# First modulation pair in single chunks, norm squares summed on TensorE, first products chunk by chunk

## The chip, the core and the metric

The kernel runs on one NeuronCore of a Trainium2 chip. The metric is the device time of one execution in microseconds (us). The engines are TensorE (PE; its weight loads are shown apart as PEld), VectorE (DVE), ScalarE (ACT), GpSimd (POOL) and SyncE (SP), which issues most of the DMA transfers.

## What is computed

Two transformer-like blocks over 512 tokens of width 1024: the first with retention, a Fourier mix and a gated feed-forward layer, the second with a gated MLP, windowed attention and 16 experts. Everything that the change touches lies in the first steps of the first block:

```python
mod = silu(c) @ w_mod + b_mod                    # 6 x 1024 columns
sh1, sc1, ... = split(mod, 6)
h  = rms_norm(x, norm1_w) * (1 + sc1) + sh1      # 512 x 1024
hc = the same for ctx (256 x 1024), with c_ctx
...
gate_f = sigmoid(h @ w_branch_gate[:, 1024:] + b)    # the first product with h
k_ctx, v_ctx = hc @ w_in[:, K and V columns]
```

## The kernel before

Activations are held transposed: 128 partitions of the model width by 512 tokens, in 8 chunks `k` of the width. Every fp32 operand of a large product is split into a high part in the matmul format and the remainder, and a product is three matmuls of 128x128 by 128x512 (`mm3`, L222 to L224: weight-high by x-high, weight-high by x-low, weight-low by x-high). The order of instructions on each engine is the order in which the code is written; nothing is rescheduled.

The first stage brings in `xin` (8 chunks in 4 DMAs), then the first four weight blocks of the gate (`wraw`, items 0 to 3, split into high and low by ScalarE and VectorE: `cH`/`cL`, `wh`/`wl`) and the modulation weights. These come in pairs: `pair_load(kp)` issues four DMAs of 512 KB, which hold shift and scale of the chunks `2kp` and `2kp+1`; `pair_mm(kp)` multiplies them on TensorE by silu(c) and silu(c_ctx) (L450) and copies the result to SBUF on ScalarE (L454); `pair_fin(kp)` sums and transposes it with eight passes on TensorE (L461) and makes `mod1` and `A1` = (1 + scale) * norm weight on VectorE (L465, L467).

The norm of x squares the chunks on ScalarE (L360, L364), adds them up on VectorE (L367), sums over partitions on TensorE (`col_sums`, L336, a product with a column of ones), takes the reciprocal root on small tiles and broadcasts it with L348 into PSUM (`pB`). `norm_pre(k)` multiplies a chunk by `pB` on VectorE (L523); `start_norm(k)` then applies scale and shift on ScalarE (L528), takes the high part in a second ScalarE pass (L530) and the remainder on VectorE (L531).

`part(c, kp)` runs the products of weight block `c` with the two chunks of pair `kp`. `warm(n)` issues n throw-away matmuls (L478, two passes each) whose only effect is that TensorE is busy; the counts come from the table `WARM0`. After the last norm, the code splits two more weight blocks and sums the squares of the context (`c1[0]`, `c1[1]`: L360, L364, L367), and behind the last products of this stage TensorE makes the context's column sums (`c1[2]`, L336). From there TensorE goes straight on to the next four blocks of the gate.

## Time and profile before

| | us |
|---|---|
| median of 3 runs (lowest to highest) | 2325.15 (2323.64 to 2325.17) |
| the profiled execution | 2323.48 |
| its span in the trace | 2321.7 |
| TensorE busy in the span | 2223.4 (96%) |
| start of the first product with h | 22.90 |
| start of the context's column sums | 57.96 |

The profiled execution is 1.78 us longer than its span and 1.67 us shorter than the median of the runs. Times in the rows below count from the start of the span. Matmul durations overlap, so the pace of a run of matmuls is read from their starts or from the chain.

### The profile page before, as it was taken

The numbers are of one execution on the slowest core, as the hardware profiler recorded it, in microseconds if no ns is written. First come the engines' busy times: TensorE is split into PE (matmuls) and PEld (weight loads), VectorE is DVE, ScalarE is ACT, GpSimd is POOL, SyncE is SP. The second block draws the span as 40 slices with busy tenths as digits, with TensorE's granted clock in tenths as the row PEclk, the third lists the DMA queues.
The fourth block names the chain that finished last, engine by engine and source line by source line (L and its number), as shares of the span: only waits on it lengthen the run. The fifth ranks groups of instructions, "written<-read, shape, count | busy, mean of one in ns | idle before, by whom it ended". The sixth has DMA issues, their size and how long they took to land.

```text
span 2321.7 us, 27993 instructions
## 1 busy us (share of the span) xinstructions
PE 2223.4 (96%) x11118; PEld 1460.6 (63%) x11118; DVE 1061.7 (46%) x2064; ACT 658.6 (28%) x1034; POOL 164.8 (7%) x304
## 2 busy tenths in 40 slices
PE   8999999999999999999999999999999989888987
PEld 6788888878888888888976785434333323332333
DVE  4645675679787865524667552111211111111112
ACT  5532234344243545332466431000000000000002
POOL 0202010101112100002211000000000000000000
PEclk9999999999999999999999999999999999999999
DMA  8647254734456544235510498999999999999998
GB/s 321 229 162 211 87 155 157 260 118 152 156 192 207 165 144 127 82 114 162 153 42 19 142 362 351 417 421 432 431 430 431 432 432 431 430 432 431 431 428 348
DMA packets 95970, 616.79 MB, mean 266 GB/s; under 512 B 12832, under 2 KB 17568, under 8 KB 75680
## 3 DMA queue, kind: packets, MB, share of 16 engines
q1 hardware_dynamic: 77136, 558.63, 60.9%
q0 software_dynamic: 18704, 56.38, 8.2%
q8 instruction: 88, 1.44, 0.3%
q14 instruction: 42, 0.34, 0.0%
HBM read 590.05 MB, written 14.94 MB: 261 GB/s over the span
## 4 chain that ended last, share of the span: by engine, by line
PE 79%; DMA 17%; DVE 2%; ACT 2%; issue 1%; POOLq 0%; SPq 0%; DVEq 0%; ACTq 0%
DMA xr<-in_w_exp_dram 16%; PE mm L224 13%; PE mm L222 13%; PE mm L223 13%; PE pgu L1817 12%; PE py L1884 6%; PE ps L1700 3%; PE b L255 2%; PE b L254 2%; PE b L253 2%; PE sm L1361 1%; PE mm L1349 1%; PE b L222 1%; PE b L223 1%; PE b L224 1%; PE ps L1731 1%
## 5 line engine op out<-in xcount | busy, mean ns | idle before, releaser
L1817 PE MATMUL pgu<-xr,xt 128*64 128x512 f32 x2032 | 463.0, 599 | 33.1 <-DMA xr<-in_w_exp_dram 32.5
L222 PE MATMUL mm<-aH,wh 128*128 128x512 f32 (+1 forms) x1104 | 420.1, 381 | 2.3 <-ACT aH L380 2.3
L223 PE MATMUL mm<-aL,wh 128*128 128x512 f32 (+1 forms) x1104 | 417.3, 378 | 0.0
L224 PE MATMUL mm<-aH,wl 128*128 128x512 f32 (+1 forms) x1104 | 417.2, 378 | 0.1
L131 DVE TENSOR_TENSOR wl<-wraw,wh 128x1024 fp32r<-128x1024 f32 (+1 forms) x212 | 256.2, 1212 | 184.6 <-ACT wh L122 184.2
L1817 PEld LDWEIGHTS pgu<-xr,xt 128*64 128x64 f32 x2032 | 143.5, 137 | 298.2 <-issue 266.8
L122 ACT ACTIVATE wh<-wraw 128x1024 fp32r<-128x1024 f32 (+1 forms) x212 | 220.1, 1044 | 262.7 <-PE mm L223 182.3
L1884 PE MATMUL py<-xr,hTe 128*64 128x512 f32 x944 | 218.2, 608 | 21.7 <-DMA xr<-in_w_exp_dram 21.7
L222 PEld LDWEIGHTS mm<-aH,wh 128*128 128x128 f32 x1104 | 208.3, 189 | 41.0 <-ACT aH L380 2.6
L224 PEld LDWEIGHTS mm<-aH,wl 128*128 128x128 f32 x1104 | 208.3, 189 | 39.3 <-DVE wl L131 0.5
L223 PEld LDWEIGHTS mm<-aL,wh 128*128 128x128 f32 x1104 | 208.4, 189 | 37.9 <-DVE aL L383 0.4
L1884 PEld LDWEIGHTS py<-xr,hTe 128*64 128x64 f32 x944 | 67.6, 139 | 139.9 <-issue 124.4
L1855 DVE TENSOR_TENSOR eg<-pgu,eg 128x512 f32<-128x512 f32 x32 | 22.1, 692 | 208.0 <-PE pgu L1817 194.7
L1807 ACT ACTIVATE hTe<-pT 128x512 f32<-128x512 f32 x32 | 19.1, 598 | 334.4 <-PE pT L1806 334.4
L1735 DVE TENSOR_TENSOR aH<-ps,aH 128x512 f32<-128x512 f32 x56 | 38.7, 692 | 121.8 <-PE ps L1732 121.8
L1705 DVE TENSOR_SCALAR xt<-ps,B,mod 128x128 f32<-128x128 f32 x32 | 11.6, 405 | 162.7 <-PE ps L1700 162.7
L108 ACT ACTIVATE yh<-y 128x512 fp32r<-128x512 f32 x15 | 9.4, 629 | 225.2 <-DVE y L1899 211.2
L1899 DVE SCALAR_TENSOR_TENSOR y<-py,sw,g2B 128x512 f32<-128x512 f32 x15 | 11.3, 750 | 135.3 <-PE py L1884 135.3
L1700 PEld LDWEIGHTS ps<-sel,xtok 128*128 128x128 f32 x496 | 57.8, 192 | 24.3 <-issue 24.3
L282 POOL DMA_DIRECT2D mraw<-in_w_adaT_dram x96 | 51.6, 537 | 302.7 <-DVE mod L297 300.7
L222 PE MATMUL mm<-gH,wh 128*128 128x512 f32 x176 | 68.5, 389 | 0.0
L223 PE MATMUL mm<-gL,wh 128*128 128x512 f32 x176 | 68.5, 389 | 0.0
(494 smaller groups left out, 3117.3 us busy)
## 6 DMA issues: line engine op xcount, KB each, us to landing
xr<-in_w_exp_dram SPq DMA_DIRECT2D x66, 4096.0 KB, 29.9
xr<-in_w_exp_dram SPq DMA_DIRECT2D x30, 2048.0 KB, 13.9
xr<-in_w_exp_dram SPq DMA_DIRECT2D x55, 1024.0 KB, 9.7
mraw<-in_w_adaT_dram POOLq DMA_DIRECT2D x96, 256.0 KB, 2.9
wraw<-in_w_up_dram SPq DMA_DIRECT2D x44, 512.0 KB, 4.0
wraw<-in_w_kv_tok_dram SPq DMA_DIRECT2D x20, 512.0 KB, 4.2
wraw<-in_w_bg_dram SPq DMA_DIRECT2D x16, 512.0 KB, 3.7
mraw<-in_w_modT_dram POOLq DMA_DIRECT2D x32, 256.0 KB, 4.8
```

The costliest lines, as they stand in the source:

```text
L122: nc.scalar.activation(h[:, :sz], r[:, :sz], AF.Copy)
L131: nc.vector.tensor_tensor(*lows.pop(0), OP.subtract)
L222: nc.tensor.matmul(ps, wh, xh, start=first, stop=False)
L223: nc.tensor.matmul(ps, wh, xl, start=False, stop=False)
L224: nc.tensor.matmul(ps, wl, xh, start=False, stop=last)
L253: nc.tensor.matmul(ps[t][:, :cols], xh[:, ts], wh[:, s], start=k == 0, stop=False)
L254: nc.tensor.matmul(ps[t][:, :cols], xl[:, ts], wh[:, s], start=False, stop=False)
L255: nc.tensor.matmul(ps[t][:, :cols], xh[:, ts], wl[:, s], start=False, stop=k == KD - 1)
L282: eng.dma_start(t, A["w_modT" if b == 1 else "w_adaT"][c, hf])
L1700: nc.tensor.matmul(pT[:, c * 128:(c + 1) * 128], xtok[:, t, k * 128:(k + 1) * 128], sel[:, t], start=t == 0, stop=t == 3)
L1817: nc.tensor.matmul(pgu[w][64 * i:64 * i + 64, :], xt[:, kq, es], t[2 * k + i], start=kq == 0, stop=kq == 7, skip_group_check=True)
L1884: nc.tensor.matmul(py[64 * hf:64 * hf + 64, :], lhs, t[2 * i + hf], start=f8 == 0 and i == 0, stop=f8 == 7 and i == 1, skip_group_check=True)
```

## The change

The first modulation pair is no longer loaded as a pair. `half_load(k)` loads shift and scale of one chunk (two DMAs of 512 KB, from a new host-side layout `w_mod0`), `half_mm(k)` multiplies them with 16 matmuls of 128 columns, `half_fin(k)` finishes one chunk with two matmuls and three small VectorE operations. The squares of x are no longer accumulated on VectorE: four chunks are squared on ScalarE and summed over partitions at once on TensorE, the other four are squared on VectorE and ScalarE, added in two pairs and then summed, all into one PSUM tile, which makes 24 matmuls with a column of ones in place of 4. The two steps of the norm are put together otherwise: VectorE now multiplies x by `A1` and `pB` in one operation (L575), ScalarE adds the shift and rounds to the high part in one pass (L578), and VectorE makes the low part from the same tile (L580). The products are written chunk by chunk of h over the weight blocks, and block 3 is split before the second pair of chunks is used. The throw-away matmuls go from 29 to 10. DMAs are issued in another order, with the same count of 512 KB tiles.

```diff
@@ -468,8 +468,37 @@
                                        V("norm1_w")[:, 2 * kp:2 * kp + 2, None].to_broadcast([128, 2, 2]),
                                        OP.add, OP.mult)
 
+    def half_load(k):
+        mt[-1 - k] = []
+        for w in range(2):
+            t = xpool.tile([128, 1024], F32, name="m0", tag="m0", bufs=5)
+            nc.sync.dma_start(t, A["w_mod0"][k, w])
+            mt[-1 - k].append(t)
+
+    def half_mm(k):
+
+        tiles = mt.pop(-1 - k)
+        p = gb()
+        for w in range(2):
+            for k8 in range(KD):
+                g = 32 * (k8 % 4)
+                nc.tensor.matmul(p[g:g + 32, w * 128:(w + 1) * 128], sil1[:, k8, :],
+                                 tiles[w][:, k8 * 128:(k8 + 1) * 128],
+                                 start=k8 < 4, stop=k8 > 3, skip_group_check=True)
+        m = xpool.tile([128, 2, 256], F32, name="modp", tag="modp", bufs=1).rearrange("p a b -> p (a b)")
+        nc.scalar.activation(m[:, :256], p[:, :256], AF.Copy)
+        return m
+
+    def half_fin(k, m):
+        p2 = smb()
+        for w in range(2):
+            nc.tensor.matmul(p2[:, 2 * w:2 * w + 2], m[:, w * 128:(w + 1) * 128], V("sel"), start=True, stop=True)
+        for w in range(2):
+            c = 8 * w + k
+            nc.vector.tensor_scalar(mod1[:, c, :], p2[:, 2 * w:2 * w + 2], V("b_mod")[:, c:c + 1], None, OP.add)
+        nc.vector.tensor_scalar(A1[:, k, :], mod1[:, 8 + k, :], 1.0, V("norm1_w")[:, k:k + 1], OP.add, OP.mult)
+
     CS = ((3, 4), (5, 6), (7,), ())
-    WARM0 = (17, 3, 1, 4, 0, 2, 2, 2)
 
     def warm(n):
 
@@ -497,39 +526,59 @@
 
     for k in range(0, KD, 2):
         nc.sync.dma_start(xin[:, k:k + 2], A["xT"][:, k:k + 2])
+    half_load(0)
     w_dma_to(1)
-    pair_load(0)
-    w_dma_to(2)
+    half_load(1)
+    w_dma_to(3)
     pair_load(1)
-    w_dma_to(3)
-    pair_load(2)
-    warm(WARM0[0])
-    ss = SumSq(L, "a")
-    for k in range(KD):
-        ss.add(xin[:, k])
+    warm(7)
+
+
     p = smb()
-    col_sums(ss.acc, 4, p)
-    nc.scalar.activation(flat(cH, 0), raws[0], AF.Copy)
-    warm(WARM0[1])
+    nc.vector.memset(p[:, :4], 0.0)
+    nsum = [0]
+
+    def sums(t_):
+        for t in range(4):
+            nc.tensor.matmul(p[:, t:t + 1], t_[:, t * 128:(t + 1) * 128], ones, start=False, stop=nsum[0] == 5,
+                             skip_group_check=True)
+        nsum[0] += 1
+
+    def square(k, tag, bufs, eng="act"):
+        t = mp.tile([128, L], F32, name="sq", tag=tag, bufs=bufs)
+        if eng == "act":
+            nc.scalar.activation(t, xin[:, k], AF.Square)
+        else:
+            nc.vector.tensor_tensor(t, xin[:, k], xin[:, k], OP.mult)
+        return t
+    s4, s5 = square(4, "nh", 2, "dve"), square(5, "nh", 2, "dve")
+    for k in range(4):
+        sums(square(k, "t2", 2))
+    s6, s7 = square(6, "ssqa", 1), square(7, "t2", 2)
+    nc.vector.tensor_tensor(s4, s4, s5, OP.add)
+    nc.vector.tensor_tensor(s6, s6, s7, OP.add)
+    sums(s4)
+    sums(s6)
     v = mean_eps(p, 4, "vx")
     r = rsqrt_(v, 4, "x")
+    nc.scalar.activation(flat(cH, 0), raws[0], AF.Copy)
+    m = half_mm(0)
     pB = gb()
     bcast(r, 4, pB)
 
     nts = {}
 
-    def norm_pre(k):
-        nts[k] = mp.tile([128, L], F32, name="nt", tag="t2", bufs=2)
-        nc.vector.tensor_tensor(nts[k], xin[:, k], pB, OP.mult)
-
-    def start_norm(k):
-        t = nts.pop(k)
-        nh = mp.tile([128, L], F32, name="nh", tag="nh", bufs=2)
-        nc.scalar.activation(nh, t, AF.Identity, scale=A1[:, k, 0:1], bias=mod1[:, k, 0:1])
-        h, l = ring()
-        nc.scalar.activation(h, nh, AF.Copy)
-        nc.vector.tensor_tensor(l, nh, h.bitcast(F32), OP.subtract)
-        hT.append((h, l))
+    def norms(*ks):
+
+        for k in ks:
+            nts[k] = mp.tile([128, L], F32, name="nt", tag="t2", bufs=2)
+            nc.vector.scalar_tensor_tensor(nts[k], xin[:, k], A1[:, k, 0:1], pB, OP.mult, OP.mult)
+        for k in ks:
+            hT.append(ring())
+            nc.scalar.activation(hT[k][0], nts[k], AF.Identity, bias=mod1[:, k, 0:1])
+        for k in ks:
+            nc.vector.scalar_tensor_tensor(hT[k][1], nts[k], mod1[:, k, 0:1], hT[k][0].bitcast(F32),
+                                           OP.add, OP.subtract)
 
     def ctx_norm(pool, cx, cH, cL, a, b):
 
@@ -573,64 +622,52 @@
 
     ps = [mmb(), mmb(), gb(), gb()]
 
-    def part(c, kp):
-        wh, wl = ws[c]
-        for k in (2 * kp, 2 * kp + 1):
-            s = slice(k * 128, (k + 1) * 128)
+    def part(k, *cs_):
+        s = slice(k * 128, (k + 1) * 128)
+        for c in cs_:
+            wh, wl = ws[c]
             mm3(ps[c], wh[:, s], wl[:, s], hT[k][0], hT[k][1], k == 0, k == KD - 1)
-    norm_pre(0)
-    norm_pre(1)
     nc.vector.tensor_tensor(flat(cL, 0), raws.pop(0), flat(cH, 0).bitcast(F32), OP.subtract)
     ws[0] = flat(cH, 0), flat(cL, 0)
     sched["ns"] = sched["nu"] = 1
-    m = pair_mm(0)
-    warm(WARM0[2])
-    pair_fin(0, m)
     w_dma_to(4)
-    start_norm(0)
-    start_norm(1)
+    half_fin(0, m)
+    m = half_mm(1)
+    pair_load(2)
+    norms(0)
     first_split(1, flat(cH, 1), flat(cL, 1))
-    for k in (2, 3):
-        norm_pre(k)
+    warm(2)
+    part(0, 0)
+    half_fin(1, m)
+    norms(1)
+    part(0, 1)
     first_split(2, *[xpool.tile([128, 1024], F32R, name="wh2", tag="wh2", bufs=2) for _ in range(2)])
-    warm(WARM0[3])
-    part(0, 0)
-    part(1, 0)
-    warm(WARM0[4])
+    part(1, 0, 1)
+    part(0, 2)
     m = pair_mm(1)
     pair_load(3)
-    w_dma_to(5)
+    w_dma_to(6)
     nc.sync.dma_start(cx, A["ctxT"])
-    part(2, 0)
-    pair_fin(1, m)
-    start_norm(2)
-    start_norm(3)
-    for k in (4, 5):
-        norm_pre(k)
-    m = pair_mm(2)
-    warm(WARM0[5])
-    part(0, 1)
-    pair_fin(2, m)
-    start_norm(4)
-    start_norm(5)
-    first_split(3, *[wpool.tile([128, 1024], F32R, name="wh", tag=t, bufs=SPLB) for t in ("wh", "wl")])
-    for k in (6, 7):
-        norm_pre(k)
-    part(1, 1)
-    part(2, 1)
-    warm(WARM0[6])
-    part(0, 2)
-    w_dma_to(6)
     nc.sync.dma_start(rope, A["rope"])
     nc.sync.dma_start(rel, A["rel"])
+    part(1, 2)
+    pair_fin(1, m)
+    norms(2, 3)
+    first_split(3, *[wpool.tile([128, 1024], F32R, name="wh", tag=t, bufs=SPLB) for t in ("wh", "wl")])
+    part(0, 3)
+    part(1, 3)
+    warm(1)
+    part(2, 0, 1)
+    m = pair_mm(2)
+    part(2, 2, 3)
+    pair_fin(2, m)
+    norms(4, 5)
+    part(3, 0, 1, 2, 3)
     m = pair_mm(3)
-    part(1, 2)
+    part(4, 0, 1, 2, 3)
     pair_fin(3, m)
-    start_norm(6)
-    start_norm(7)
-    part(2, 2)
-    for kp in range(3):
-        part(3, kp)
+    norms(6, 7)
+    part(5, 0, 1, 2, 3)
     w_split_to(6)
     c1[0]()
     c1[1]()
@@ -638,8 +675,8 @@
     nc.sync.dma_start(cr, A["cr"].to_broadcast([128, D]))
     nc.gpsimd.tensor_copy(tb[:, 1:2], A1[:, 6, 0:1])
     bg_load(3)
-    for c in range(4):
-        part(c, 3)
+    part(6, 0, 1, 2, 3)
+    part(7, 0, 1, 2, 3)
     c1[2]()
     nc.scalar.activation(sg, cr, AF.Sigmoid)
     nc.vector.tensor_tensor(cr, cr, sg, OP.mult)
@@ -2020,6 +2057,8 @@
     A["ctxT"] = tT(x["ctx"][0])
     A["ctxT_2"] = tT(x["ctx_2"][0])
     wi = x["w_in"][0]
+    wm = x["w_mod"][0][:, :2048].reshape(1024, 2, 1024)
+    A["w_mod0"] = np.stack([[tile_tok(wm[:, w, k * 128:k * 128 + 128], 8, 128)[0, 0] for w in range(2)] for k in range(2)])
     A["w_mod"] = tile_tok(x["w_mod"][0][:, :2048], 4, 256)
     rows = lambda w: np.ascontiguousarray(w.T.reshape(48, 128, 2, 512).transpose(0, 2, 1, 3))
     A["w_modT"] = rows(x["w_mod"][0])
```

The order in which TensorE gets its instructions, from the start of the program to the first product, before (`b<-vecs,ident` are throw-away matmuls, `sm<-ones,ssq` the column sums, `b<-ident,rs` the broadcast, `m_*` tiles of the modulation weights):

```order
L478 MATMUL b<-vecs,ident 128x256 x17
L336 MATMUL sm<-ones,ssq 128x1 x4
L478 MATMUL b<-vecs,ident 128x256 x3
L348 MATMUL b<-ident,rs 128x128 x4
L450 MATMUL b<-m_126,sil_114 32x256 x4
L450 MATMUL b<-m_128,sil_114 32x256 x4
L450 MATMUL b<-m_130,sil_114 32x256 x4
L450 MATMUL b<-m_132,sil_114 32x256 x4
L478 MATMUL b<-vecs,ident 128x256
L461 MATMUL sm<-vecs,modp 128x2 x4
L478 MATMUL b<-vecs,ident 128x256 x4
L222 MATMUL mm<-aH,cH 128x512
```

The same stretch of TensorE with the change:

```order
L507 MATMUL b<-vecs,ident 128x256 x7
L543 MATMUL sm<-ones,sq 128x1 x24
L485 MATMUL b<-m_124,sil_114 32x128 x8
L485 MATMUL b<-m_126,sil_114 32x128 x8
L348 MATMUL b<-ident,rs 128x128 x4
L495 MATMUL sm<-vecs,modp 128x2 x2
L485 MATMUL b<-m_130,sil_114 32x128 x8
L485 MATMUL b<-m_132,sil_114 32x128 x8
L507 MATMUL b<-vecs,ident 128x256 x2
L222 MATMUL mm<-aH,cH 128x512
```

The column sums have grown from 4 to 24 matmuls, they stand ahead of everything else, and the throw-away matmuls that stood between them and the first product are gone but for two.

ScalarE from the first copy of a modulation result to the fourth weight block with the change (`modp` are those copies, `aH` the high parts of h, `cH`, `wh_298` and `wh` the high parts of weight blocks 1, 2 and 3):

```order
L489 ACTIVATE modp<-b 128x256 x2
L578 ACTIVATE aH<-nt,mod_71 128x512
L108 ACTIVATE cH<-wraw 128x1024
L578 ACTIVATE aH<-nt,mod_71 128x512
L108 ACTIVATE wh_298<-wraw 128x1024
L454 ACTIVATE modp<-b 128x512
L578 ACTIVATE aH<-nt,mod_71 128x512 x2
L108 ACTIVATE wh<-wraw 128x1024
```

Both copies of the single chunks stand ahead of the first `aH`, and block 3 (`wh`) comes right behind chunks 2 and 3 of h, where it came behind chunks 4 and 5 before.

TensorE around the second pair with the change (`wh_298`, `wh_299` are block 2, `wh` block 3, `mm<-aH,cH` blocks 0 and 1):

```order
L450 MATMUL b<-X_97,sil_114 32x256 x4
L222 MATMUL b<-aH,wh_298 128x512
L223 MATMUL b<-aL,wh_298 128x512
L224 MATMUL b<-aH,wh_299 128x512
L461 MATMUL sm<-vecs,modp 128x2 x4
L222 MATMUL b<-aH,wh 128x512
L223 MATMUL b<-aL,wh 128x512
L224 MATMUL b<-aH,wh 128x512
L222 MATMUL b<-aH,wh 128x512
L223 MATMUL b<-aL,wh 128x512
L224 MATMUL b<-aH,wh 128x512
L507 MATMUL b<-vecs,ident 128x256
```

Block 3's products with chunks 0 and 1 now stand directly behind the finish of this pair (L461), ahead of every product with chunks 2 and 3.

## Rows read from the trace of the kernel before

**Rows 1.** The page, parts 1 (engines) and 4 (chain that ended last).
```profile
PE 2223.4 (96%) x11118; PEld 1460.6 (63%) x11118; DVE 1061.7 (46%) x2064; ACT 658.6 (28%) x1034; POOL 164.8 (7%) x304
...
PE 79%; DMA 17%; DVE 2%; ACT 2%; issue 1%; POOLq 0%; SPq 0%; DVEq 0%; ACTq 0%
```
**Rows 2.** Stretches: busy time of each engine, granted clock, DMA share, GB/s.
```profile
22.90:26.50 3.60, 2.86 (x9) 1.36 (x9) 2.66 (x4) 3.21 (x4) 0.00 (x0) 1.00 1.02 419
...
51.00:57.00 6.00, 6.00 (x27) 4.86 (x27) 5.12 (x10) 4.23 (x10) 0.00 (x0) 1.00 0.62 214
```
**Rows 3.** TensorE in order of time: start, us, line, operation, count, idle before.
```profile
3.66 9.10 PE L478 MATMUL b<-vecs,ident 128*128 128x256 f32 x34 [3.66 <-DMA ident<-in_ident_dram]
13.73 1.05 PE L336 MATMUL sm<-ones,ssq 128*128 128x1 f32 x8 [0.97 <-DVE ssq L367]
...
16.08 1.16 PE L348 MATMUL b<-ident,rs 128*128 128x128 f32 x8
17.17 1.93 PE L450 MATMUL b<-m,sil 128*32 128x256 f32 x32
...
19.82 1.05 PE L461 MATMUL sm<-vecs,modp 128*128 128x2 f32 x8
20.74 1.97 PE L478 MATMUL b<-vecs,ident 128*128 128x256 f32 x8
22.90 0.50 PE L222 MATMUL mm<-aH,cH 128*128 128x512 f32 x1 [0.19 <-ACT aH L530]
...
27.61 0.64 PE L450 MATMUL b<-m,sil 128*32 128x256 f32 x8
...
57.96 0.50 PE L336 MATMUL sm<-ones,ssq 128*128 128x1 f32 x4
```
**Rows 4.** ScalarE in order of time, the same columns.
```profile
21.38 0.81 ACT L528 ACTIVATE nh<-nt,mod,A 128x512 f32<-128x512 f32 x1 [1.60 <-DVE A L467]
22.22 0.63 ACT L530 ACTIVATE aH<-nh 128x512 fp32r<-128x512 f32 x1
...
24.13 1.04 ACT L108 ACTIVATE cH<-wraw 128x1024 fp32r<-128x1024 f32 x1
...
65.10 0.37 ACT L553 ACTIVATE cB<-sm 128x256 f32<-128x256 f32 x1
```
**Rows 5.** VectorE in order of time, the same columns.
```profile
17.28 1.28 DVE L523 TENSOR_TENSOR nt<-xin,b 128x512 f32<-128x512 f32 x2 [1.25 <-DMA m<-in_w_mod_dram]
...
22.88 0.69 DVE L531 TENSOR_TENSOR aL<-nh,aH 128x512 fp32r<-128x512 f32 x1 [1.54 <-ACT aH L530]
...
25.20 1.23 DVE L109 TENSOR_TENSOR cL<-wraw,cH 128x1024 fp32r<-128x1024 f32 x1 [0.26 <-ACT cH L108]
...
50.36 0.69 DVE L531 TENSOR_TENSOR aL<-nh,aH 128x512 fp32r<-128x512 f32 x1 [0.68 <-ACT aH L530]
...
53.59 3.59 DVE L367 TENSOR_TENSOR ssq<-ssq,sq 128x256 f32<-128x256 f32 x7
```
**Rows 6.** Groups by line and shape: busy us, mean ns.
```profile
L1899 DVE SCALAR_TENSOR_TENSOR y<-py,sw,g2B 128x512 f32<-128x512 f32 x15 | 11.3, 750 | 135.3 <-PE py L1884 135.3
...
L659 ACT ACTIVATE grt<-mm,vecs 128x512 f32<-128x512 f32 x7 | 4.8, 688 | 17.7 <-PE mm L224 17.7
```
**Rows 7.** Stretches around two later falls of the granted clock.
```profile
498.00:505.00 7.00, 6.14 (x14) 4.54 (x15) 5.65 (x9) 6.84 (x11) 0.00 (x0) 0.50 0.00 0
...
1392.00:1396.00 4.00, 4.00 (x36) 3.90 (x34) 1.20 (x4) 2.26 (x4) 0.00 (x0) 1.00 0.57 197
1396.00:1400.00 4.00, 4.00 (x13) 3.29 (x13) 2.06 (x11) 1.60 (x3) 0.00 (x0) 0.58 1.01 424
```
**Rows 8.** TensorE in order of time, at the two later places.
```profile
494.69 1.89 PE L348 MATMUL sm<-ident,rs 128*128 128x128 f32 x8 [1.38 <-DVE rs L330]
...
1392.48 0.95 PE L1577 MATMUL mm<-ones,ssq 128*128 128x1 f32 x8
1393.29 1.04 PE L1566 MATMUL sm<-wr,xtok 128*128 128x16 f32 x8
```

## The prediction

> **What bounds the kernel now.** I read the page first: TensorE is busy 96% of the span and holds 79% of the chain that ended last, so a microsecond saved or lost ahead of TensorE's stream moves the end by as much [rows 1]. Then the stretches and the order of time for the first 60 us, the only part that the change touches. TensorE does throw-away work, column sums, broadcast and the first pair until 22.90, when the first product with h starts; it is held there by ScalarE's high part [rows 3]. From 22.90 to 26.50 it is busy 2.86 of 3.60 us, from 51 to 57 all the time [rows 2]. At 57.96 it makes the context's column sums [rows 3] and goes on with products. So the question is by how much that 57.96 moves. I walk through the new order with durations of this trace, first at the full clock, then ask for the clock. The sum is made against the profiled execution (2323.48 us, its span and 1.78 us around it); the median of the runs lies 1.67 us above it.
>
> **The walk at full clock.**
>
> *Throw-away work and sums.* 34 passes took 9.10 us and ended at 12.76; eight later ones took 1.97, 0.23 each without the tail [rows 3]. Without the last 20 (4.6 us) they end at 8.2. Four sums of 128x1 are eight passes and take 1.05 us, about 1.0 in a row [rows 3]; six such groups follow each other on TensorE, 8.2 to 14.2, and the squares are ready in time. Before, the sums ended at 14.78. VectorE's adds (0.69 each) are gone from the path, but TensorE has taken their place: 0.6 us gained.
>
> *half_mm.* It has 32 passes like pair_mm, with half the columns. Bounds: 1.93 us, as pair_mm [rows 3], or 1.0, if it goes with the columns. I take 1.7, nearer to the row with the same number of passes, so 14.2 to 15.9. Its two tiles are the fifth and sixth of the 512 KB stream, which runs at 419 GB/s [rows 2], 1.25 us a tile; the ninth came at about 17.2 before, when pair_mm began [rows 3], so these are there at 13.4. The root (1.3 us from the sums' end to the broadcast, 14.78 to 16.08 [rows 3]) is hidden under it. Broadcast 1.16: 17.05. half_fin, four passes: 0.50, as the last of rows 3: 17.55.
>
> The Trainium skill ("TensorE: Matmul & The Clock Gate", Part 1, "Wait — 56ns, not 53.3ns?") gives some 62 ns per matmul as a floor of the sequencer in one decoding mode. By that floor a half_mm would last an estimated 1.98 us and the sum would grow by 0.6; pair_mm's 32 passes, 1.93 us with the tail [rows 3], stay just under it.
>
> *First product.* mod1 and A1 take 0.5 us (from 20.87, the end of L461, to 21.38 [rows 3, 4]): 18.05. Multiplying by A1 and pB is a two-scalar operation not seen here in this form; 0.75 by L1899 [rows 6] (0.64 if it costs what L523 does [rows 5]): 18.8. But ScalarE's order has the second half_mm's copy ahead: half_mm(1) runs 17.55 to 19.25, its copy of 256 columns takes 0.37 [rows 4]: 19.7. Then the single pass for the high part, 0.69 by L659 (0.63 as L530, 0.81 as L528) [rows 4, 6], in place of 0.81 + 0.63: first product at 20.4, 2.5 us earlier than before.
>
> *To the second pair.* Low part 0.75: 21.15; third product and half_fin(1) until 22.2. VectorE does block 1's low part, 1.23 [rows 5], 21.3 to 22.55, then A1 for chunk 1 (23.05), multiply (23.8); high part 24.5, low part 25.25, block 2's high (1.04 [rows 4]) 25.4 and low 26.65. TensorE waits for these three times, 22.8 to 24.5 the longest, and starts pair_mm(1) at 27.1 with 15 products done. Before: 27.61 with 12 done [rows 3]. The lead is 0.5 us and three products (0.7). The pair's last tile is the fifteenth, at 24.7: no wait.
>
> *The wait at block 3.* pair_mm(1) takes 1.87 us (1.93 with the tail [rows 3]), three products 0.8, pair_fin(1) 0.8: TensorE is free at 30.6. Its next product wants block 3's high part. That stands on ScalarE behind aH of chunks 2 and 3, which wait for VectorE's two multiplies, which wait for pair_fin(1): 31.15 (A1), 32.55 (two multiplies), 33.25 (second aH, 0.69), 34.2 (split 1.04, 0.1 of it overlapped). TensorE stands idle 3.65 us and then 0.8 us more for the low part (1.23). Before, block 3 was used last and its split was hidden. At 36.4 there are 24 products done.
>
> *To the end.* 72 products at 0.23, two pair_mm and pair_fin at 1.87 and 0.8, one warm (0.43) and some restarts: 23.0 us, 59.4. The last pair's chain gives its low part at about 54.35; before, that was 51.05, and the sums of squares of the context, behind two splits, ended at 57.18, 6.13 later [rows 5]. So they end at 60.5 now, TensorE waits 1.1 us for them, and the column sums start at 60.5 in place of 57.96: **+2.5 us**. With the bounds of half_mm, the multiply and the high part: +1.2 to +3.3. Cheaper norms and 19 throw-away matmuls less are thus given back at block 3 and at the context.
>
> **The clock.** Until now TensorE had 512- or 256-column work all along. With the change, it has nothing but 128x1 sums for 6 us (8.2 to 14.2). This trace shows such a place: from 1392.48 TensorE ran 128x1 and 128x16 matmuls back to back, was busy 4.00 of 4.00 us, and at 1396 the granted clock fell to about half: mean 0.58 over the next 4 us, though 128x256 matmuls ran again [rows 7, 8]. After another such norm the clock was 0.50 (1.2 GHz) from 498 to 505, with products in sequence most of that time: 14 in 6.14 us busy, 0.44 each [rows 7], against 27 in 6.00, some 0.23, at the full clock [rows 2]. The broadcast took 1.89 there against 1.16 [rows 3, 8]. I therefore expect the lower level from some point in the sums on. What it costs:
>
> - to the first product: two half_mm, 1.2 more each (0 if bound by issue, 1.7 if doubled), broadcast 0.7, half_fin 0.4: 3.5 us. First product at 23.9, later than the 22.90 of before.
> - to the second pair: some ten products and half_fin on the path, each 0.2 longer, less slack: 2.0.
> - pair_mm(1), three products, pair_fin(1): 2.9, all ahead of the chain of block 3.
> - after the 3.65 us of idleness there, the lower level again for some 3.3 to 6.2 us of products, which then do half the work: 1.7 to 3.1, say 2.4.
>
> All four make 10.8. If the full clock returns under half_mm and broadcast, the first is 2.0, the second and third nothing: 4.4. Between these ends I take 7.5: 2323.48 + 2.5 + 7.5 = 2333.5 in the profile, **2335** as a median; this case's own range is 2332 to 2338.5.
>
> **Rivals.**
>
> *The clock stays up.* For it: the gap from 12.76 to 13.73 with the sums behind it did no harm before, and the new sums come with dense weight loads. Against it: the stretch at 1392 is of the same kind. Then only the walk counts: 2325.15 + 2.5 = 2327.7, no measurable change. The Trainium skill (same page, "Why this matters for your kernels") asks only that TensorE has no idle gaps between bursts of matmuls. By that rule this rival would win, since the sums leave no gap; rows 7 and 8 speak against it, for there was none at 1392 either. Chance 0.22.
>
> *Faster: block 3 is ready.* If its high part is there when pair_fin(1) ends at 30.6 and not at 34.2, and the small waits go as well, TensorE runs through from the first product: 20.4 + 96 products (22.2) + three pair_mm (5.6) + finishes (2.9) + 0.4 = 51.5 in place of 57.96, 2318.7 us. It needs 4.65 of these 6.4 us to show, so the wait at block 3 must fall below about 1 us and the clock must hold. ScalarE's written order speaks against it. Chance 0.06.
>
> *The change does not reach the path.* If the single chunks arrive late, for instance because the stream starts slower, half_mm waits as pair_mm did at 17.2 and the first product stays near 22.9, with the clock kept by other work: about +1.25 us for the one tile more ahead of pair 1, and +2.5 at most: 2326.4 to 2327.7. For it: the stream is full (DMA share 1.02 [rows 2]). Against: the tiles come first now. Chance 0.06.
>
> **How the numbers follow.** The falling clock gets 0.66; nearly all of it is slower by over 0.2% (4.65 us, about what a measurement of this kernel can tell from no change; the border is 2329.8). Same: 0.22 + 0.06 = 0.28. Faster: 0.06. The range of 8 in 10 reaches down over most of the unchanged cases, to 2324, and up past the sum of all bounds (2325.15 + 2.5 + 10.8 = 2338.5) to 2340.
>
> **What the changed profile would show.** 128x1 sums between about 8 and 14, first product at 20 (full clock) to 24; a granted clock of 0.50 in parts of 12 to 40; a wait of TensorE of 3 to 4 us for ScalarE's wh of block 3 between 30 and 40; the context's column sums at 60 (full) to 72, waiting for ssq. I am wrong if the clock column stays at 1.00 through the sums, if TensorE does not wait at block 3, or if the column sums start before 57.96.

## The result and the profile after

| | before | after |
|---|---|---|
| median of 5 runs each (us) | 2325.15 (2323.64 to 2325.53) | 2338.76 (2333.98 to 2347.24) |
| ratio of the runs, 95% interval | | 1.0068 [1.0056, 1.0080] |
| the profiled execution, its span | 2323.48, 2321.7 | 2338.76, 2337.0 |
| first product with h starts | 22.90 | 20.14 |
| context's column sums start | 57.96 | 65.63 |

The change makes the kernel slower. By the ratio it costs 15.8 us (0.0068 x 2325.15; 13.0 to 18.6 by the interval), by the medians 13.6. The forecast was +9.85, and its range ended at +14.85. The direction and most of the mechanisms in the first 66 us were as forecast; the size was not. Two slow runs of the kernel before, 4318.86 and 5755.45 us, beside experiments 5 to 8 are left out of the ratios there.

The page after, parts 1 (engines) and 4 (the chain that ended last), which answer to [rows 1]:

```profile
PE 2234.3 (96%) x11152; PEld 1468.5 (63%) x11152; DVE 1061.7 (45%) x2065; ACT 651.7 (28%) x1025; POOL 165.2 (7%) x304
...
PE 77%; DMA 17%; DVE 2%; ACT 2%; issue 1%; POOL 0%; SPq 0%; POOLq 0%; DVEq 0%; ACTq 0%
```

TensorE is still the bound. It is busy 10.9 us longer with 34 more passes; the mean granted clock of this execution is 0.985, of the one before 0.992, so most of that is likely the same work at a lower clock. TensorE in order of time, as in [rows 3] (start, us, line, operation, count, idle before and its releaser):

```profile
3.61 4.93 PE L507 MATMUL b<-vecs,ident 128*128 128x256 f32 x14 [3.61 <-DMA ident<-in_ident_dram]
8.38 5.47 PE L543 MATMUL sm<-ones,sq 128*128 128x1 f32 x48
13.78 1.93 PE L485 MATMUL b<-m,sil 128*32 128x128 f32 x32
15.64 1.91 PE L348 MATMUL b<-ident,rs 128*128 128x128 f32 x8
...
17.82 1.08 PE L485 MATMUL b<-m,sil 128*32 128x128 f32 x32
...
20.14 0.51 PE L222 MATMUL mm<-aH,cH 128*128 128x512 f32 x1 [0.17 <-ACT aH L578]
...
24.41 0.79 PE L222 MATMUL mm<-aH,cH 128*128 128x512 f32 x1 [1.56 <-ACT aH L578]
...
37.30 0.50 PE L222 MATMUL b<-aH,wh 128*128 128x512 f32 x1 [3.66 <-ACT wh L108]
...
38.56 0.80 PE L224 MATMUL b<-aH,wh 128*128 128x512 f32 x1 [0.38 <-DVE wh L109]
...
65.63 0.58 PE L336 MATMUL sm<-ones,ssq 128*128 128x1 f32 x4 [1.64 <-DVE ssq L367]
...
236.87 0.63 PE L867 MATMUL mm<-ident,kd 128*128 128x128 f32 x4 [2.17 <-issue]
```

The granted clock by stretch (stretch, its length, TensorE busy and matmuls, clock, DMA share, GB/s):

```profile
8.38:11.00 2.62, 2.62 (x25) 1.00 1.03 417
11.00:13.78 2.78, 2.78 (x26) 1.00 1.03 421
13.90:17.10 3.20, 3.20 (x39) 0.50 1.03 420
...
24.50:30.90 6.40, 6.40 (x29) 0.50 0.82 336
...
38.00:41.00 3.00, 2.62 (x8) 0.50 1.04 429
```

The reader is to see three things. First, after 5.5 us of one-column sums without a gap the clock is at its lower level (0.50, 1.2 GHz) from 13.9 to 17.1. It goes there again behind the waits of 1.56 us (at 24.41) and 3.66 us (at 37.30). Second, the first product comes 2.8 us earlier than before, and still the column sums come 7.67 us later. Third, there is a wait far behind the head: at 236.87 TensorE waits 2.17 us for its transposes of `kd`, the packed k of the retention, where it had waited 0.27 us before. The clock falls behind that too:

```profile
236.00:238.00 2.00, 1.13 (x9) 0.99 (x10) 0.46 (x1) 1.96 (x4) 0.00 (x0) 1.00 0.05 20
238.00:240.00 2.00, 2.00 (x11) 1.61 (x10) 1.61 (x4) 0.11 (x1) 0.00 (x0) 0.78 0.00 0
240.00:242.00 2.00, 2.00 (x6) 1.57 (x5) 1.72 (x3) 0.00 (x0) 0.00 (x0) 0.50 0.00 0
```

(Here the columns are busy time and instructions of TensorE, its weight loads, VectorE, ScalarE and GpSimd, then clock, DMA share and GB/s.) Matching the two traces product by product gives the lag, the time by which the same product starts later than before. With the places given in the time of the kernel before, it is 7.7 us at the column sums, 6.1 at 106 (a 1.16 us wait of the kernel before at 100 is gone, so a delay gives something back there), 8.0 at the transposes of k, 9.6 at 243, 10.6 at 510, 14.4 at 1443, and 15.3 at the end of the span.

### The profile page after: what moved, and what is told of

The parts are those of the page before. It is cut to its first block, busy times and chain, and to the rows that moved or that the text cites. A ratio compares the mean times of both kernels' runs of the same rounds, so it can differ in the third digit from the quotient of the medians.

```text
span 2337.0 us, 28055 instructions
## 1 busy us (share of the span) xinstructions
PE 2234.3 (96%) x11152; PEld 1468.5 (63%) x11152; DVE 1061.7 (45%) x2065; ACT 651.7 (28%) x1025; POOL 165.2 (7%) x304
## 4 chain that ended last, share of the span: by engine, by line
PE 77%; DMA 17%; DVE 2%; ACT 2%; issue 1%; POOL 0%; SPq 0%; POOLq 0%; DVEq 0%; ACTq 0%
DMA xr<-in_w_exp_dram 16%; PE mm L222 13%; PE mm L224 13%; PE mm L223 13%; PE pgu L1854 11%; PE py L1921 7%; PE ps L1737 3%; PE b L255 1%; PE sm L1398 1%; PE b L254 1%; PE b L253 1%; PE mm L1386 1%; PE b L222 1%; PE b L224 1%; PE b L223 1%
## 5 line engine op out<-in xcount | busy, mean ns | idle before, releaser
L1742 DVE TENSOR_SCALAR xt<-ps,B,mod 128x128 f32<-128x128 f32 x32 | 11.6, 406 | 161.8 <-PE ps L1737 161.8
## 6 DMA issues: line engine op xcount, KB each, us to landing
xr<-in_w_exp_dram SPq DMA_DIRECT2D x55, 1024.0 KB, 10.9
```

## The experiments

My theory was that one-column sums take the clock down, that the fourth block's split holds TensorE, and that the delay of the head reaches the end one to one. The rivals were that the sums are harmless, that the parts are bound by transfers, and that a delay costs more than itself. The context's column sums (57.96 before, 65.63 after) are the measure of the head. Ratios are to the kernel before on the same chip; experiments 1 to 4, 5 to 8 and 9 to 12 ran on three different chips.

**1 and 2. Sums by 128 columns, the fourth block's split early, each alone.** Edits of the changed kernel:

```diff
-    nc.vector.memset(p[:, :4], 0.0)
+    nc.vector.memset(p, 0.0)
+    ones_w = xpool.tile([128, 128], F32, name="ones_w")
+    nc.vector.memset(ones_w, 1.0)
...
-            nc.tensor.matmul(p[:, t:t + 1], t_[:, t * 128:(t + 1) * 128], ones, start=False, stop=nsum[0] == 5,
-                             skip_group_check=True)
+            nc.tensor.matmul(p[:, t * 128:(t + 1) * 128], t_[:, t * 128:(t + 1) * 128], ones_w, start=False,
+                             stop=nsum[0] == 5, skip_group_check=True)
...
-    v = mean_eps(p, 4, "vx")
+    v = mp.tile([128, 4], F32, name="vx", tag="vx", bufs=2)
+    nc.vector.tensor_scalar(v, p[:, 0:512:128], 1.0 / D, EPS, OP.mult, OP.add)
```

```diff
     part(0, 2)
+    first_split(3, *[wpool.tile([128, 1024], F32R, name="wh", tag=t, bufs=SPLB) for t in ("wh", "wl")])
     m = pair_mm(1)
...
     norms(2, 3)
-    first_split(3, *[wpool.tile([128, 1024], F32R, name="wh", tag=t, bufs=SPLB) for t in ("wh", "wl")])
```

> The changed kernel with one edit: each of the 24 sums multiplies by 128 columns of ones in place of one column, so TensorE streams 128 columns per pass in the same places; the sums themselves are the same. Theory (the granted clock falls because the sums leave TensorE's array nearly empty): the clock is 1.00 through 8 to 20 us, half_mm and broadcast take 1.1 and 1.16 us in place of 1.93 and 1.91, the first product starts near 19.3 us in place of 20.14, and the time falls by 1 to 5 us below the changed kernel's, to about 2334 to 2338. Rival (the clock falls because of what comes before or after, or at any new kernel start): the clock falls near 14 as before and the time stays within 1 us of the changed kernel's.

> The changed kernel with weight block 3 split ahead of the second pair (ScalarE's and VectorE's two operations moved up, nothing else). Theory (the 3.67 us of idleness at block 3 costs itself and half-clock work behind it): that wait is gone or below 1 us, the clock does not fall near 37 us, the context's column sums start 4 to 7 us earlier than the changed kernel's 65.63 us, and the time is 4 to 8 us below it. Rival (the wait only moves to chunks 2 and 3 of h, whose high parts come 2 us after pair_fin): TensorE waits some 2 us there, and the gain is 2 us or less.

Measured: 2336.20 us, ratio 1.0047 [1.0033, 1.0060], with 128 columns; 2333.49, 1.0037 [1.0023, 1.0050], with the early split. With 128 columns the clock stayed up through the sums and the first product came at 19.39, but the waits of 1.6 and 3.7 us took it down later, and the column sums came at 64.83. With the early split the 3.66 us wait was gone and the column sums came at 62.68, though the clock fell already near 10.9 in that execution and the first product came at 23.45. So each is a cost of the head, and neither alone is most of it. By the runs alone this is clear for the split, whose interval lies below that of the changed kernel; the interval of the wide sums overlaps it. The early split brought the column sums 3 us forward, where 4 to 7 had been expected.

**3. Both.** 

> Both edits, wide sums and block 3 split early, in the changed kernel. If the two costs are separate, the gains add: column sums of the context near 57 to 60 us, time 2323 to 2329, near the kernel before. If the wait between the first two chunks (1.56 us idle near 23) lowers the clock by itself, it still falls near 24 us and the time stays above 2329.

Measured: 2326.04 (12 runs), ratio 1.0008 [0.9999, 1.0017]; first product 20.38, column sums 59.54 with 1.21 us of waiting for the context's squares. The two edits together take back 14 of the 15.8 us: nearly all of the loss hangs on the clock and the split. The clock still fell at 26.6, behind the 1.56 us wait, as the second case of the expectation had it, but the time did not stay above 2329.

**4. A plain delay.** The kernel before, with throw-away matmuls at the end of the head, at the full clock:

```diff
+    warm(18)
     c1[2]()
```

> The kernel before with one edit: 18 throw-away matmuls (7.7 us at full clock) directly ahead of the context's column sums, so that TensorE reaches that place at about 65.7 us, as in the changed kernel, with the clock up and nothing else moved. Theory (a delay of the head costs more than itself, because something behind it then comes late, such as the transfer that TensorE waits for near 235 us): the time grows by 10 to 15 us. Rival (a delay costs itself, or less, and what came on top in the changed kernel is chance): it grows by 5.5 to 8 us, to 2331 to 2333.

Measured: 2336.60, ratio 1.0050 [1.0035, 1.0064], that is +11.6 us, with the column sums at 66.00, 8.0 late. A delay that has nothing to do with the change cost 3.6 us more than itself, which is about half the width of its interval. In its profile the transposes of k waited 2.63 us; in those of experiments 1 to 3 they waited 4.3, 2.2 and 2.7. The third is the telling one. It was level with the kernel before when k was packed, and the last transfer was issued at the same time. GpSimd issuing it, and TensorE's transposes, first in the trace of the kernel before, then in that of experiment 3:

```profile
222.81 0.52 POOL L401 DMA_DIRECT2D kd<-kd  x1 [7.03 <-DMA kd<-rr]
...
228.87 0.63 PE L830 MATMUL mm<-ident,kd 128*128 128x128 f32 x4 [0.27 <-PE b L255]
```

```profile
222.68 0.52 POOL L401 DMA_DIRECT2D kd<-kd  x1 [6.95 <-DMA kd<-rr]
...
231.34 1.03 PE L870 MATMUL mm<-ident,kd 128*128 128x128 f32 x4 [2.74 <-issue]
```

The transposes ran by 228.87 in one execution and not before 231.34 in the other. `pack_twice` packs q and k by eight transfers and then makes a second copy by one transfer out of the first, which waits until all eight have landed (some 7.0 us in these rows). In the kernel before the last transfer is back just as TensorE comes for it.

The time of that last transfer from its issue to its landing, in the kernel before, in after, in 3, and in 8 (below):

```profile
DMA to landing us min/median/max: 5.6/5.6/5.6
...
DMA to landing us min/median/max: 8.0/8.0/8.0
...
DMA to landing us min/median/max: 8.3/8.3/8.3
...
DMA to landing us min/median/max: 5.4/5.4/5.4
```

So it is not the delay in itself that makes the copy late. In after it was issued 5.7 us later than before (228.48 against 222.81) and TensorE came 6.1 us later, so the slack was as it had been; the copy took 8.0 us in place of 5.6. Experiment 3 had the long copy without a lag (0.0 there), 8 the short one with a lag of 3.3. In the five executions with a long copy the last five of its 80 packets started one by one, 5.25 to 7.34 us behind the issue; in the four with a short one all had started by 4.73. The profiled execution of 3 is the slowest of its twelve runs (2334.30 us, median 2326.04), so most of its runs can't have lost as much.

**5 and 6. Without the chain of transfers.** Both copies are packed from the source, in the kernel before and in the changed one (the edit also reaches the two later places that call `pack_twice`):

```diff
     pack(eng, dst, src)
-    eng.dma_start(dst[64:128], dst[0:64])
+    pack(eng, dst, src, base=64)
```

> The kernel before, with one edit far behind the head: the two copies of q and of k are each packed straight from their source by eight transfers, where the second copy used to be one transfer out of the first and so waited for it. Theory (a late k copy is what a delay of the head runs into): in the profile of before the transposes of k waited 0.27 us only, so 2320 to 2325, no wait at that line. Rival (the copy is not the cause of anything): 2323 to 2326, as before.

> The changed kernel with the same edit. Theory: the 2.17 us wait at the transposes of k and the clock fall behind it are gone, about 4 us: 2333 to 2335, so 10 us above the kernel before with this edit instead of 13.6. Rival (the excess behind the head comes from clock falls elsewhere, at 500 and at 1400): the wait is gone, but the distance to the kernel before with this edit stays 12 to 14 us.

Measured: the kernel before stays the same (2323.76, ratio 0.9999 [0.9989, 1.0008]), which both its expectations allow; the changed one takes 2335.78 (4 runs), ratio 1.0048 [1.0033, 1.0064]. Its loss falls from 15.8 to 11.2 us, and the wait for k is gone in both profiles. The fall of 4.6 us is the size of the theory, but the two intervals overlap, and the distance of the two kernels, 11.4 us by the ratios and 12.0 by the medians, lies between the 10 of the theory and the 12 to 14 of the rival. The runs alone don't decide. The profile of the sixth adds something that I had not asked for. TensorE in order of time, and two stretches:

```profile
8.83 8.05 PE L543 MATMUL sm<-ones,sq 128*128 128x1 f32 x48
16.81 1.93 PE L485 MATMUL b<-m,sil 128*32 128x128 f32 x32
18.68 2.08 PE L348 MATMUL b<-ident,rs 128*128 128x128 f32 x8
...
21.33 1.93 PE L485 MATMUL b<-m,sil 128*32 128x128 f32 x32
...
24.70 0.69 PE L222 MATMUL mm<-aH,cH 128*128 128x512 f32 x1
...
38.97 0.79 PE L222 MATMUL b<-aH,wh 128*128 128x512 f32 x1 [3.66 <-ACT wh L108]
...
68.51 0.58 PE L336 MATMUL sm<-ones,ssq 128*128 128x1 f32 x4 [1.64 <-DVE ssq L367]
...
238.76 0.60 PE L867 MATMUL mm<-ident,kd 128*128 128x128 f32 x4
```

```profile
12.00:16.00 4.00, 4.00 (x20) 0.50 1.02 417
16.00:24.00 8.00, 8.00 (x83) 0.50 1.03 418
```

The head is the same code as in the changed kernel. In this execution the clock fell inside the sums and stayed low through both half_mm, so the first product came at 24.70 and the column sums 10.55 us late. The lag then was 10.3 at 147, 10.7 at 1403, and 10.6 at the end of the span (2332.3 against 2321.7). With k out of the way the head's delay arrived at the end, in sum: the clock fell again behind the wait of 1.64 us and added 1.7, and places where the kernel before had waited gave 1.8 back (at 100 and at k).

**7. The head mended further.** Experiment 3 with the context's squares between two splits, the straight packing, and the fourth block's split directly ahead of `norms(2, 3)` instead of ahead of the pair:

```diff
-    w_split_to(6)
+    w_split_to(5)
     c1[0]()
     c1[1]()
+    w_split_to(6)
```

> The changed kernel with the sums by 128 columns of ones, the fourth block's split early, the squares of the context ahead of the second of two splits, and the two copies packed straight. Theory: the head ends 1 us earlier than with the first two edits (column sums of the context at 58.3 to 58.6, before 57.96), and no wait for k: 2321 to 2324, level with the kernel before or up to 3 us under it. Rival (the square sums are late for another reason, or the k copy is no cost): 2325 to 2327.

Measured: 2324.16 (11 runs), ratio 0.9997 [0.9988, 1.0006], level with the kernel before. The wait for the squares is gone. But the column sums came at 59.55, a microsecond later than I had expected, for the wait for the fourth block's low part was back (1.0 us) and the 1.56 us wait had stayed.

**8. One part of the change alone: the squares summed on TensorE, in the kernel before.** The sums block of the changed kernel in place of `SumSq` and `col_sums`, with seven throw-away matmuls ahead of it.

> The kernel before with one part of the change alone: the squares of x summed over partitions on TensorE by chunk, 24 products of one column for each four, instead of being added up on VectorE first; norm, order and loads as before. Theory (the sums pay only if the clock holds): the factor's spread to all rows starts at about 14 instead of 16.08, but the clock falls there to half as in the changed kernel, and the first pair of modulation waits for its transfer; first product 22 to 23.5, 2323 to 2327. Rival (the sums are a gain by themselves): first product at 20.5 to 21, column sums of the context about 2 us earlier, 2320 to 2323.

Measured: 2328.98 (10 runs), ratio 1.0020 [1.0010, 1.0029]: +4.7 us. The expected span of times for the first theory was too low. Its fall of the clock is there; the wait for the first pair's transfer is not. TensorE, two stretches of its clock, and the one wait of TensorE in the stretch 220 to 330:

```profile
9.17 7.78 PE L513 MATMUL sm<-ones,sq 128*128 128x1 f32 x48
...
27.49 0.51 PE L222 MATMUL mm<-aH,cH 128*128 128x512 f32 x1 [0.20 <-ACT aH L550]
```

```profile
12.00:17.00 5.00, 5.00 (x25) 0.50 1.03 420
17.00:22.00 5.00, 5.00 (x22) 0.50 1.03 421
```

```profile
PE mm L850 <- DMA kd<-kd: 1.8, 1, 1.8
```

The sums ended at 16.95, not at 14, and everything up to 22 ran at the lower clock: first product 27.49, column sums 62.54, 4.6 us late. The last row names the releaser that the view of after could only call "issue": the second copy of k, here that of the second batch of heads. The first batch did not wait.

**9. The delay again, with k packed straight.** Experiments 4 and 5 together.

> The kernel before with 18 throw-away matmuls ahead of the context's column sums (a delay of 8.0 us in an earlier profile, which cost 11.6 us in the median) and both copies of q and k packed straight. Theory (a delay costs itself, and what was on top of it was the late second copy of k with the clock fall behind it): 2331 to 2333, 8 us above the kernel before. Rival (a delayed stream costs more than itself whatever k does, by clock falls or transfers elsewhere): 2335 to 2337.

Measured: 2330.44 (12 runs), ratio 1.0025 [1.0016, 1.0034], +5.8 us, with the column sums 7.5 late, a lag of 6.9 at 107 (the wait at 100 gives its part back), and no wait for k. The same delay cost 11.6 with the chain of transfers, on another chip. The theory holds in the runs and the rival falls. The profiled execution, at 2333.08 us one of the two slowest of the twelve, lost 3 us more behind 243.

**10. The wait behind the first product shortened and filled.** Experiments 1, 2 and 5 and the context's squares as in 7, with this:

```diff
     norms(0)
+    warm(2)
+    half_fin(1, m)
+    nts[1] = mp.tile([128, L], F32, name="nt", tag="t2", bufs=2)
+    nc.vector.scalar_tensor_tensor(nts[1], xin[:, 1], A1[:, 1, 0:1], pB, OP.mult, OP.mult)
     first_split(1, flat(cH, 1), flat(cL, 1))
-    warm(2)
+    hT.append(ring())
+    nc.scalar.activation(hT[1][0], nts[1], AF.Identity, bias=mod1[:, 1, 0:1])
+    nc.vector.scalar_tensor_tensor(hT[1][1], nts[1], mod1[:, 1, 0:1], hT[1][0].bitcast(F32),
+                                   OP.add, OP.subtract)
     part(0, 0)
-    half_fin(1, m)
-    norms(1)
+    warm(4)
     part(0, 1)
```

> The changed kernel with all that has been mended so far (sums by 128 columns, the fourth block's split ahead of the second pair, context squares between two splits, straight packing), and the wait behind the first product shortened and filled: the second chunk's modulation is finished ahead of the first product, its multiply stands ahead of the second block's split on VectorE, and four throw-away matmuls follow the first products. Theory (what is left at the head is the 1.56 us wait and the half clock that follows it): no half clock from 20 to 32, column sums of the context at 56.5 to 58, 2321 to 2323. Rival (the end of the head is set by the pairs' transfers): column sums at 59 as before this edit, 2323.5 to 2325.

Measured: 2321.51 (12 runs), ratio 0.9988 [0.9978, 0.9997]. The interval just excludes no change. TensorE in order of time, and its clock:

```profile
9.51 5.67 PE L545 MATMUL sm<-ones_w,sq 128*128 128x128 f32 x48
15.12 1.08 PE L485 MATMUL b<-m,sil 128*32 128x128 f32 x32
...
20.25 0.48 PE L222 MATMUL mm<-aH,cH 128*128 128x512 f32 x1
...
55.51 0.58 PE L336 MATMUL sm<-ones,ssq 128*128 128x1 f32 x4
```

```profile
9.50:15.20 5.70, 5.70 (x53) 1.00 1.03 423
15.20:25.00 9.80, 9.24 (x103) 1.00 1.02 415
25.00:42.00 17.00, 16.58 (x137) 1.00 1.02 416
```

The clock is at its full level all through and no wait above 0.3 us is left between 18 and 66. The column sums come at 55.51, 2.45 us earlier than before. The rival, that transfers set the end of the head, falls: it had the column sums at 59, and the DMA share is as full as ever (1.02).

**11 and 12. Parts of the change alone, in the kernel before: sums by 128 columns; the two-step norm.**

> The kernel before with the squares summed on TensorE by chunk, but by 128 columns of ones instead of one. Theory (the loss of 4.8 us with one column was the clock): the clock stays at 1.00 through the sums, the broadcast starts 0.5 us later to 1 us earlier than 16.08, and the time is that of the kernel before, 2323 to 2325.5. Rival (the sums on TensorE cost by themselves, since they take the place of throw-away work only in part): 2327 to 2330, as with one column.

> The kernel before with the two-step norm alone: one multiply by A1 and the factor on VectorE after the modulation is known, then the high part in one pass on ScalarE. Theory: per pair the chain from A1 to the first high part is 0.75 + 0.7 in place of 0.81 + 0.63, so the first product stays within 0.3 us of 22.90 and the time within 2 us of the kernel before, 2322 to 2326. Rival (the chain is longer, since the multiply was done ahead before): each of four pairs loses 0.7 to 1.5 us where TensorE waits for it, 2326 to 2329.

Measured: 2323.61 (12 runs), 0.9999 [0.9989, 1.0009], with the clock at 1.00 through the sums and column sums at 58.40; and 2321.97 (12 runs), 0.9991 [0.9981, 1.0001], with column sums at 56.62. TensorE's sums and the clock in 11:

```profile
9.56 5.67 PE L515 MATMUL sm<-ones_w,sq 128*128 128x128 f32 x48
```

```profile
9.50:15.30 5.80, 5.80 (x52) 5.68 (x51) 2.54 (x5) 3.25 (x5) 0.00 (x0) 1.00 1.02 417
```

So the sums on TensorE are neither gain nor loss where the clock holds. With one column (8) they lost 4.7, and the two intervals do not touch: the two kernels differ only in the columns of the sums and in how their result is read. The two-step norm may be a small gain: 1.3 us at the head in the profile, and an interval that touches no change.

## Why the prediction was right on the head and wrong on the size

- **Throw-away work and sums.** Forecast 8.2 to 14.2, measured 8.38 to 13.85 where the clock held until 13.8. Right there; in experiment 6 the clock was down by 12 and they ran from 8.83 to 16.88.
- **half_mm.** At the full clock it took 1.08 us, at the lower one 1.93. I took 1.7 for the full clock, by the number of passes, and the lower of my bounds was right. For the lower clock I had 2.9 (1.7 and 1.2 more), so that was 1.0 too much. The Trainium skill ("TensorE: Matmul & The Clock Gate", Part 1, "Wait — 56ns, not 53.3ns?") gives the floor of some 62 ns per matmul for one decoding mode only. It does not bind here: 32 passes in 1.08 us is 34 ns each.
- **First product.** Forecast 20.4 with the clock up and 23.9 with it down; measured 19.39 (experiment 1, up), 20.14 (after, down for 3.2 us only), 24.70 (experiment 6, down from within the sums). Right to about a microsecond.
- **The clock.** It fell within or right behind the sums in each execution with one column that was profiled here (after, experiments 2, 6 and 8). With 128 columns it stayed up through them each time (1, 3, 7, 10, 11). The Trainium skill (same page, "Why this matters for your kernels") asks for no idle gaps; the sums have none, and the clock fell. By that rule the change would have made no measurable difference, as the rival had it. The traces agree with it behind the wait of 3.66 us, where the clock fell each time (after, 1 and 6). Behind the wait of 1.56 us it fell in five of the six profiles that have it (not in 6); the prediction had no term for that fall. So the rival's price for a clock that stays up through the sums, 2.5 us, was too low as well: experiment 1 had its clock up through them and lost 10.9.
- **The wait at block 3.** Forecast 3.65 us, measured 3.66, twice. The wait for the context's squares was forecast as 1.1 and was 1.64. Both mechanisms are as written.
- **The sum for the head.** Forecast +10.0 (2.5 + 7.5), with 4.4 to 10.8 for the clock; measured +7.67 in one execution and +10.55 in another of the same head. Less the 2.5 of the walk, the clock's term would be 5.2 and 8.1, within its bounds. But no run shows the 2.5 by itself, and the parts were not those of the sum: the full case had 3.5 up to the first product, which in after came even before the 20.4 of the full clock, and the fall behind the 1.56 us wait came in its place. The size of the head is right in part by luck.
- **The step that failed** is the first one: "a microsecond saved or lost ahead of TensorE's stream moves the end by as much". The sum had no term behind 57.96, and the profile of after lost 7.6 us there, as much again as at the head. Of this, 3.5 us came at the transposes of k, where the copy took 8.0 us in place of 5.6: 1.9 of waiting and 1.6 from the clock that falls behind it. Places where the kernel before had waited gave 1.6 back, and the rest came behind 243. The table sets the loss of the runs against the delay of the head in the one profile of each (us; a loss is known to 2 or 3 us):

| | delay of the head | loss by the ratio | more than the delay | copy of k to landing |
|---|---|---|---|---|
| after | 7.67 | 15.8 | 8.1 | 8.0 |
| 1 | 6.87 | 10.9 | 4.0 | 8.2 |
| 2 | 4.72 | 8.6 | 3.9 | 8.3 |
| 3 | 1.58 | 1.9 | 0.3 | 8.3 |
| 4 | 8.04 | 11.6 | 3.6 | 8.1 |
| 8 | 4.58 | 4.7 | 0.1 | 5.4 |
| 6, straight | 10.55 | 11.2 | 0.6 | |
| 7, straight | 1.59 | -0.7 | -2.3 | |
| 9, straight | 7.51 | 5.8 | -1.7 | |
| 10, straight | -2.45 | -2.8 | -0.3 | |

  With the chain of transfers, delays of 4.7 us and more cost some 4 us on top in 1, 2 and 4, and 8.1 in after (5.3, if its head is taken as the 10.55 of experiment 6). With straight packing a delay cost itself, to within some 2 us. That is the price, known to a few us only, as the intervals with and without the chain overlap or nearly touch (1.0068 and 1.0048 for the changed kernel, 1.0050 and 1.0025 for the plain delay) and were taken on different chips. That the delay brings the long copy about is not shown: 3 had it without a lag there, and 8, on another chip, was delayed and had neither the long copy nor the extra cost.
- **What is left.** The profiled execution of after gains 4.7 us more lag between 510 and the end. A good part of it is the clock in places where it falls in most traces here, by a different amount each time. The stretches behind two norms, in after and then in the kernel before:

```profile
500.00:520.00 20.00, 15.07 (x55) 0.66 0.08 34
...
1400.00:1440.00 40.00, 38.89 (x174) 0.87 0.71 279
```

```profile
490.00:510.00 20.00, 14.88 (x60) 0.74 0.10 38
...
1390.00:1430.00 40.00, 38.39 (x196) 0.96 0.78 307
```

  Experiment 6 shows 0.74 and 0.96 again, as the kernel before, with the changed head. So this difference need not come from the change; these profiles show no more than that it varies.

The likeliest case of the forecast, the falling clock, is the one that came.

**Open.** Why the second copy of k takes 8.0 to 8.3 us in five executions (after and 1 to 4) and 4.8 to 5.6 in four (before, 8, 11 and 12) was not found. The five share neither the lag nor the kernel. Experiments 1 to 4 share a chip, so the chip is a rival that was not tried. Whether the kernel before, unchanged, ever waits there is not known either. Its runs are no faster with straight packing, so it can't do so often; but 8 of its 35 runs beside experiments 9 to 12 took over 2328 us (median 2323.16), which no profile explains.

## What to carry to other kernels

A delay at the head need not reach the end one to one. So look along the whole stream for transfers whose result is used as it lands (here a wait of 0.27 us that ended a chain of two transfers), see how much their time varies, and give them a term with an upper bound. Work that keeps TensorE busy is not all alike to its clock: 48 passes of one column in a row were followed by the lower clock in four of four profiles, the same sums by 128 columns in none of five. When the order on TensorE is changed, walk the orders of ScalarE and VectorE too: one split that stood behind a norm cost a wait of 3.66 us, and a lower clock behind it.

## What the runs showed of the hardware

- 48 passes of 128x128 by one column took 5.47 us while the clock held for most of them and 8.05 us when it fell inside; with 128 columns they took 5.67 (5.69 once), and the clock stayed at 1.00 in all five profiles.
- The same instructions were run at different clocks in different executions: the first product of the same head came at 20.14 and at 24.70. So one profile of such a stretch does not size a clock fall.
- 32 passes of 128 columns, which go in turn to four groups of 32 output partitions, took 1.08 us at the full clock, 34 ns each, and 1.93 at the lower one.
- One and the same transfer of 512 KB inside SBUF took 4.8 to 8.3 us from issue to landing. Issued at 222.81 it took 5.6 us, issued at 222.68 in another execution 8.3.
